# Latent attention scores: three products over 96 or 97 rows of the array become two over 128 rows and one over 33, and the small ones of two key blocks stand on the two halves of the array's rows

## Chip, core and metric

The kernel runs on one core of a Trainium2 chip. What counts is the device time of one execution, in microseconds (us); lower is better. PE is TensorE (matrix products), PEld its weight loads, ACT ScalarE, DVE VectorE, POOL GpSimd, SP the engine whose queue issues most of the DMAs (SPq).

## The reference

A trunk of two encoder layers over 2048 tokens of width 1024. The part that this case is about is the attention of the second layer (8 heads, one rotary key shared by all heads):

```
def mla_attention(q_nope, q_rope, k_nope, k_rope, v):      # per head: 64 + 32 columns, v 64
    scale = (C_NOPE + C_ROPE) ** -0.5                      # 96 ** -0.5
    ...
        s = (jnp.einsum('bqhd,bshd->bhqs', qn, k_nope)
             + jnp.einsum('bqhr,bsr->bhqs', qr, k_rope)).astype(jnp.float32) * scale
        pr = jax.nn.softmax(s, axis=-1).astype(v.dtype)
        return jnp.einsum('bhqs,bshd->bqhd', pr, v)
```

Everything around it (input projections, the windowed attention of the first layer, the gates, the output projections with layer norm) is the same in both kernels.

## The kernel before

Numbers are kept in two parts, a rounded high part (fp32r) and the rest as a low part; a product of two such numbers is high x high + high x low + low x high. `kn`, `kr`, `qn`, `qr` are the plain and the rotary columns of keys and queries in DRAM, index 0 the high part and 1 the low part.

`phase_d` is the attention. Its outer loop runs over 32 **query blocks** `blk` = head x chunk of 512 queries (four chunks to a head), its inner loop over 16 **key blocks** `kb` of 128 keys. In each key block:

- PE makes the scores of 128 keys x 512 queries in a PSUM tile `pst` (4 buffers) by three products: `kh` x `qh` with 97 rows (64 plain, 32 rotary, and a 97th row that adds minus the row maximum of the queries), `kh` x `ql` and `kl` x `qh` with 96 rows each (L1320 to L1322).
- ACT takes the exponential in place (L1323) and the rounded copy `ph` (L1326); DVE takes the rest `pl` (L1328); POOL adds `ph` to `acc`, the sum of the weights (L1334).
- PE makes one product `pm` (L1195) for the row maximum of the query block two further on, and DVE reduces it (L1196).
- PE makes the two value products `px` and `py` (L1245, L1246) of the key block `LAG` = 4 earlier.

So PE has six products of 512 columns per key block. Once in a query block come further: at `kb` = 5 the maxima of the next query block are transposed (`pmt`, L1205), turned round by ACT into `mt`, written to DRAM (`mrow`) and read back as row 96 of `qh` for the next query block (the DMA `mqh<-mrow`, last line of `mla_max_end`). The finished `px` and `py` of the query block before are copied by ACT (`oa`, `ob`) and written out (`yc`, and the last row to `sums`); `acc` of the block before is split by ACT and POOL into `acs`, summed on PE by two products `psum`, and its row `srow` goes out on SP as well.

Once in a head come the loads of the next head (`mla_load_qk`, `mla_load_v`): all go through SP's queue, in the order in which a scheduler put them there. The tiles `qh`, `ql`, `kh`, `kl` and `mv` stand twice, for even and odd heads, so these loads start when the last query block of the head before lets go of its tiles, that is at the first query block of a head, and they are for the head after it. The order of PE in `phase_d` is that of the code (`manual_schedule`); the other engines and SP's queue are put in order by the scheduler.

Of the kernel before, what the change touches and what calls it, by code (L numbers as in the profile page):

```python
# [11 lines left out]
F32 = mybir.dt.float32  # L12
F32R = mybir.dt.float32r
I32 = mybir.dt.int32
AF = mybir.ActivationFunctionType
# [5 lines left out]
P = 128  # L21
S = 2048
D = 1024
KT = D // P
CH = 512
# [4 lines left out]
LAG = 4  # L30
# [24 lines left out]
class Builder:  # L55
# [1109 lines left out]
    def _mla_qk(self, es, b, side):  # L1165
        tc, nc = self.tc, self.nc
        out = []
        for nm in ("qh", "ql", "kh", "kl"):
            p = es.enter_context(tc.tile_pool(name=f"m{nm}{b}", bufs=1, side=side))
            out.append(p.tile([97, S], F32R, name=f"m{nm}{b}"))  # L1170
        nc.scalar.activation(out[2][96:97], self.c["ones"][0:1, 0:1].broadcast_to([1, S]), AF.Copy)
        return out

    def mla_load_qk(self, h):
        d = self.d
        qh, ql, kh, kl = self.mla_qk[h % 2]
        for part, (q, k) in enumerate(((qh, kh), (ql, kl))):
            self.dma(k[0:64], d["kn"][64 * h:64 * h + 64, part])
            self.dma(k[64:96], d["kr"][:, part])
            self.dma(q[0:64], d["qn"][64 * h:64 * h + 64, part])  # L1180
            for a in range(2):
                r = 128 * (h // 4) + 64 * a + 16 * (h % 4)
                self.dma(q[64 + 16 * a:80 + 16 * a], d["qr"][r:r + 16, part])

    def mla_max(self, blk, s):

        nc, c = self.nc, self.c
        h, qc = divmod(blk, 4)
        qh, ql, kh, kl = self.mla_qk[h % 2]
# [5 lines left out]
        nc.tensor.matmul(ps, qh[0:96, q0:q0 + P], kh[0:96, kc * CH:(kc + 1) * CH], start=True, stop=True)  # L1195
        nc.vector.tensor_reduce(self.mx[blk][:, b, kc:kc + 1], ps, AX.X, ALU.max)  # L1196

    def mla_max_end(self, blk):
        nc, c = self.nc, self.c
        h, qc = divmod(blk, 4)  # L1200
# [3 lines left out]
        ps = self.psC("pmt")  # L1204
# [15 lines left out]
    def phase_d(self):  # L1220
# [9 lines left out]
        phr = Ring(es, tc, "mph", LAG + 3)  # L1230
        plr = Ring(es, tc, "mpl", LAG + 2)
        sp = es.enter_context(tc.tile_pool(name="mla", bufs=1))
        vs = self.mla_v
# [14 lines left out]
        def finish(h, qc, x, y):  # L1248
# [4 lines left out]
            ox = sp.tile([P, CH], F32, name="oa", tag="oa", bufs=2)  # L1253
            nc.scalar.activation(ox, x, AF.Copy)
            oy = sp.tile([P, CH], F32, name="ob", tag="ob", bufs=2)
# [11 lines left out]
        def total(h, qc, hl):  # L1267
# [3 lines left out]
            row = sp.tile([P, CH], F32, name="srow", tag="ob", bufs=2)[0:1]  # L1271
# [25 lines left out]
        with tc.manual_schedule(engines={mybir.EngineType.PE}):  # L1297
            for blk in range(NBLK):
                h, qc = divmod(blk, 4)
                qh, ql, kh, kl = self.mla_qk[h % 2]  # L1300
# [15 lines left out]
                for kb in range(16):  # L1316
                    with tc.high_priority(100) if blk == 0 and kb < LAG else ExitStack():
                        ps = self.ps.tile([P, CH], F32, name="pst", tag="W", bufs=4)
                        ks = slice(kb * P, (kb + 1) * P)
                        mm(ps, kh[0:97, ks], qh[0:97, qs], start=True, stop=False)  # L1320
                        mm(ps, kh[0:96, ks], ql[0:96, qs], start=False, stop=False)  # L1321
                        mm(ps, kl[0:96, ks], qh[0:96, qs], start=False, stop=True)  # L1322
# [14 lines left out]
                        if kb == MAX_AT and old is not None and blk + 1 < NBLK:  # L1337
                            self.mla_max_end(blk + 1)
                        queue.append((x, y, vs[h % 2], kb, ph, pl))
# [129 lines left out]
```

## Time and profile before

| | |
|---|---|
| median of 3 runs | 2878.97 us (2873.27 to 2884.52) |
| the profiled execution | 2881.51 us, span of its instructions 2879.7 us |
| PE busy, share of the span | 2819.8 us, 98% |
| PEld, DVE, ACT, POOL busy | 2292.0, 1987.6, 1322.2, 1096.7 us |
| mean granted TensorE clock | 0.991 |
| attention (first `pst` product to the last) | 1682.7 to 2430.9 us of the span |

"Busy" is the time in which an engine has an instruction under way. A PE product of 512 columns shows as 0.40 us, but the next one starts long before it ends, so the distance from start to start is its cost in a row of products. The clock is a share of 2.4 GHz: 1.00 is 2.4 GHz, 0.50 is 1.2 GHz.

### The profile page before, as it was taken

To read this page: it belongs to the slowest core of one execution; us is meant where nothing else is said; L and a number is where in the kernel's file an instruction comes from. 1 tells how busy PE (TensorE), PEld (TensorE's weight loads), DVE (VectorE), ACT (ScalarE), POOL (GpSimd) and SP (SyncE) were. 2 spreads that over 40 slices of the span, in tenths; PEclk is the share of its full clock that TensorE was granted. 3 is DMA by queue.
4 is the path that set the end of the run, shared out by engine and by line. 5 is a ranking of instruction groups with operands and counts; after the bars stand their busy time and mean duration, and the time that the engine had idled before them with its cause. 6 is when DMAs were issued, how large, how long until landed. Compare 5 with 4: busy or idle time off the path is not lost. (4 is left out here: it accounts for less than half of the span.)

```text
span 2879.7 us, 38354 instructions
## 1 busy us (share of the span) xinstructions
PE 2819.8 (98%) x12808; PEld 2292.0 (80%) x12808; DVE 1987.6 (69%) x3957; ACT 1322.2 (46%) x2475; POOL 1096.7 (38%) x833
## 2 busy tenths in 40 slices
PE   9999999999999999999999999999999999899999
PEld 7888888888788887888887877777777776678887
DVE  4688557786655554454764789989898995666665
ACT  3545335445211111324442368888888887211111
POOL 0011000022311111120102258898899888523432
PEclk9999999999999999999999999999999999899999
DMA  7644365453733445423873333133322323433441
GB/s 233 186 139 140 124 194 166 133 142 118 219 119 119 130 136 212 148 66 128 292 268 108 106 101 76 37 72 84 84 54 61 83 69 78 139 106 114 126 123 43
DMA packets 316598, 365.26 MB, mean 127 GB/s; under 512 B 33248, under 2 KB 244368, under 8 KB 311280
## 3 DMA queue, kind: packets, MB, share of 16 engines
q1 hardware_dynamic: 249056, 295.62, 36.6%
q10 hardware_dynamic: 67344, 67.18, 7.0%
q8 instruction: 101, 1.65, 0.2%
q14 instruction: 97, 0.79, 0.1%
HBM read 238.19 MB, written 124.53 MB: 126 GB/s over the span
## 5 line engine op out<-in xcount | busy, mean ns | idle before, releaser
L1334 POOL TENSOR_TENSOR acc<-acc,ph 128x512 f32<-128x512 f32 x448 | 582.9, 1302 | 41.8 <-ACT ph L1326 10.9
L1328 DVE TENSOR_TENSOR pl<-pst,ph 128x512 fp32r<-128x512 f32 x512 | 347.0, 684 | 62.7 <-ACT ph L1326 50.0
L1196 DVE TENSOR_REDUCE mx<-pm 128x1 f32<-128x512 f32 x512 | 347.8, 682 | 27.4 <-PE pm L1195 21.1
L78 PE MATMUL pa<-xh,w 128*128 128x512 f32 x832 | 328.4, 395 | 6.0 <-ACT xh L68 6.0
L79 PE MATMUL pa<-xl,w 128*128 128x512 f32 x832 | 329.9, 397 | 0.0
L80 PE MATMUL pa<-xh,w 128*128 128x512 f32 x832 | 328.0, 394 | 0.0
L1323 ACT ACTIVATE pst<-pst 128x512 f32<-128x512 f32 x512 | 296.6, 585 | 61.2 <-PE pst L1322 29.9
L1326 ACT ACTIVATE ph<-pst 128x512 fp32r<-128x512 f32 x512 | 301.5, 595 | 31.8 <-POOL acc L1334 1.6
L78 PE MATMUL py<-wh,ou 128*128 128x512 f32 x512 | 208.3, 407 | 13.0 <-DVE ox L639 8.2
L1320 PE MATMUL pst<-mqh,mkh 97*128 97x512 f32 x512 | 205.6, 402 | 3.6 <-DVE pl L1328 1.9
L1195 PE MATMUL pm<-mkh,mqh 96*128 96x512 f32 x512 | 203.3, 398 | 4.8 <-DVE mx L1196 4.8
L647 POOL TENSOR_TENSOR ox<-ox,ln_g 128x1024 f32<-128x1024 f32 x32 | 80.4, 2514 | 334.3 <-DMA praw<-in_pT 171.6
L90 PE MATMUL pg<-wh,oht 128*128 128x512 f32 x512 | 201.1, 393 | 4.5 <-ACT oht L68 4.5
L1245 PE MATMUL px<-ph,mv 128*128 128x512 f32 x512 | 205.3, 401 | 0.0
L79 PE MATMUL py<-wl,ou 128*128 128x512 f32 x512 | 205.3, 401 | 0.0
L1321 PE MATMUL pst<-mql,mkh 96*128 96x512 f32 x512 | 204.4, 399 | 0.0
L1322 PE MATMUL pst<-mqh,mkl 96*128 96x512 f32 x512 | 203.8, 398 | 0.0
L80 PE MATMUL py<-wh,ou 128*128 128x512 f32 x512 | 203.6, 398 | 0.0
L1246 PE MATMUL py<-pl,mv 128*66 128x512 f32 x512 | 201.9, 394 | 0.8 <-DVE pl L1328 0.7
L90 PE MATMUL pg<-wl,oht 128*128 128x512 f32 x512 | 200.4, 391 | 0.0
L671 ACT ACTIVATE osg<-pg 128x512 f32<-128x512 f32 x64 | 38.3, 599 | 344.8 <-PE pg L92 333.2
L78 PEld LDWEIGHTS pa<-xh,w 128*128 128x128 f32 x832 | 157.4, 189 | 37.8 <-ACT xh L68 7.0
(370 smaller groups left out, 6255.3 us busy)
## 6 DMA issues: line engine op xcount, KB each, us to landing
ou<-u SPq DMA_DIRECT2D x96, 256.0 KB
qw<-q SPq DMA_DIRECT2D x64, 256.0 KB
x1T<-oxt ACTq DMA_DIRECT2D x64, 256.0 KB
cx<-x1T SPq DMA_DIRECT2D x16, 1024.0 KB
q<-st SPq DMA_DIRECT2D x32, 256.0 KB
u<-ua SPq DMA_DIRECT2D x32, 256.0 KB
wraw<-in_w_out SPq DMA_DIRECT2D x16, 512.0 KB
ox<-in_x SPq DMA_DIRECT2D x16, 512.0 KB
```

The source lines that it names most:

```text
L78: mm(ps, ah, bh, start=start, stop=False)
L79: mm(ps, ah, bl, start=False, stop=False)
L80: return mm(ps, al, bh, start=False, stop=stop)
L90: mm(ps, a[:, 0, k], b[k][part][:, cols], start=k == 0 and part == 0, stop=False)
L1196: nc.vector.tensor_reduce(self.mx[blk][:, b, kc:kc + 1], ps, AX.X, ALU.max)
L1245: mm(x, v[:, kb, 0:P], ph, start=kb == 0, stop=kb == 15)
L1320: mm(ps, kh[0:97, ks], qh[0:97, qs], start=True, stop=False)
L1321: mm(ps, kh[0:96, ks], ql[0:96, qs], start=False, stop=False)
L1323: ex = nc.scalar.activation(ps, ps, AF.Exp, scale=scale)
L1326: nc.scalar.activation(ph, ps, AF.Copy)
L1328: behind = nc.vector.tensor_tensor(pl, ps, pf, ALU.subtract)
L1334: nc.gpsimd.tensor_tensor(acc, acc, pf, ALU.add)
```

## The change

The scores need 64 x 3 + 32 x 3 + 1 = 289 rows of products. The change lays them out as 128 + 128 + 33:

- `k1` x `q1`, 128 rows: plain high x high (64), rotary high x high (32), rotary low x high (32; the high rotary queries stand twice in `q1`).
- `k2` x `q2`, 128 rows: plain high x low (64), plain low x high (64).
- `k3` x `q3`, 33 rows: rotary high x low (32) and the row of minus the maximum (1). `k3` is loaded once and for all heads, even key blocks on partitions 0 to 32 and odd ones on 64 to 96. `q3` holds the 512 queries of one query block on both partition ranges, two buffers, filled by six DMAs per query block (`mla_load_q3`), two of them from `mrow`.

The key blocks are taken in pairs: both products of 128 rows of the even block, the two of 33 rows one after the other (the even block's on rows 0 to 63 of the array, the odd block's on rows 64 to 127, each in the PSUM tile of its own block), then both of the odd block. In the built program the two small ones are marked as tiles of 64 rows at row 0 and row 64, all other products of the loop as 128 rows at row 0.

To make room, the ring of `ph` goes from 7 to 6 buffers, and `oa` and `ob` (with `srow`, which shares the buffer) from two buffers to one.

```diff
     def mla_load_qk(self, h):
...
+        self.dma(k1[0:64], d["kn"][hs, 0])
+        for part in range(2):
+            self.dma(k1[64 + 32 * part:96 + 32 * part], d["kr"][:, part])
+        self.dma(q1[0:64], d["qn"][hs, 0])
+        for copy in range(2):
             for a in range(2):
                 r = 128 * (h // 4) + 64 * a + 16 * (h % 4)
-                self.dma(q[64 + 16 * a:80 + 16 * a], d["qr"][r:r + 16, part])
+                o = 64 + 32 * copy + 16 * a
+                self.dma(q1[o:o + 16], d["qr"][r:r + 16, 0])
+        for part in range(2):
+            self.dma(k2[64 * part:64 * part + 64], d["kn"][hs, part])
+            self.dma(q2[64 * part:64 * part + 64], d["qn"][hs, 1 - part])
...
+    def mla_load_q3(self, blk):
+
+        h, qc = divmod(blk, 4)
+        q3 = self.mla_q3[blk] = self.mla_q3_pool.tile([97, CH], F32R, name="mq3", tag="mq3", bufs=2)
+        for u in range(2):
+            for a in range(2):
+                r = 128 * (h // 4) + 64 * a + 16 * (h % 4)
+                o = 64 * u + 16 * a
+                self.dma(q3[o:o + 16], self.d["qr"][r:r + 16, 1, qc * CH:(qc + 1) * CH])
+            self.dma(q3[64 * u + 32:64 * u + 33], self.d["mrow"][blk])
...
-        mrow = self.d["mrow"][blk]
-        self.dma(mrow.rearrange("o (b t) -> (o b) t", b=4), mt)
-        self.dma(self.mla_qk[h % 2][0][96:97, qc * CH:(qc + 1) * CH], mrow)
+        self.dma(self.d["mrow"][blk].rearrange("o (b t) -> (o b) t", b=4), mt)
...
-        phr = Ring(es, tc, "mph", LAG + 3)
+        phr = Ring(es, tc, "mph", LAG + 2)
...
-            row = sp.tile([P, CH], F32, name="srow", tag="ob", bufs=2)[0:1]
+            row = sp.tile([P, CH], F32, name="srow", tag="ob", bufs=1)[0:1]
...
-                        ps = self.ps.tile([P, CH], F32, name="pst", tag="W", bufs=4)
-                        ks = slice(kb * P, (kb + 1) * P)
-                        mm(ps, kh[0:97, ks], qh[0:97, qs], start=True, stop=False)
-                        mm(ps, kh[0:96, ks], ql[0:96, qs], start=False, stop=False)
-                        mm(ps, kl[0:96, ks], qh[0:96, qs], start=False, stop=True)
+                        def whole(ps, kb, start):
+                            ks = slice(kb * P, (kb + 1) * P)
+                            mm(ps, k1[:, ks], q1[:, qs], start=start, stop=False)
+                            mm(ps, k2[:, ks], q2[:, qs], start=False, stop=not start)
+
+                        if kb % 2 == 0:
+                            pair = [self.ps.tile([P, CH], F32, name="pst", tag="W", bufs=4) for _ in range(2)]
+                            whole(pair[0], kb, True)
+                            for u in range(2):
+                                r = slice(64 * u, 64 * u + 33)
+                                mm(pair[u], k3[r, kb // 2], q3[r], start=u == 1, stop=u == 0)
+                            whole(pair[1], kb + 1, False)
+                        ps = pair[kb % 2]
```

PE's order in the middle of a query block. Before, one key block (`mqh`, `mql`, `mkh`, `mkl` are the tiles `qh`, `ql`, `kh`, `kl`, the number behind a name is its buffer):

```order
L1320 MATMUL pst<-mqh_13506,mkh_13514 128x512
L1321 MATMUL pst<-mql_13510,mkh_13514 128x512
L1322 MATMUL pst<-mqh_13506,mkl_13518 128x512
L1195 MATMUL pm<-mkh_14407,mqh_14399 128x512
L1245 MATMUL px<-ph_15387,mv_13637 128x512
L1246 MATMUL py<-pl_15388,mv_13637 66x512
```

And now on PE, a pair of key blocks (`mq_13506`, `mq_13510` are `q1`, `q2`; `mk_13514`, `mk_13518` are `k1`, `k2`; the row with x2 is the two small products, from `q3` and `k3`):

```order
L1354 MATMUL pst<-mq_13506,mk_13514 128x512
L1355 MATMUL pst<-mq_13510,mk_13518 128x512
L1362 MATMUL pst<-mq_14470,mk_14458 128x512 x2
L1354 MATMUL pst<-mq_13506,mk_13514 128x512
L1355 MATMUL pst<-mq_13510,mk_13518 128x512
L1226 MATMUL pm<-mk_13514,mq_13506 128x512
L1276 MATMUL px<-ph_14697,mv_13636 128x512
L1277 MATMUL py<-pl_14698,mv_13636 66x512
L1226 MATMUL pm<-mk_13514,mq_13506 128x512
L1276 MATMUL px<-ph_14708,mv_13636 128x512
L1277 MATMUL py<-pl_14709,mv_13636 66x512
```

It is twelve products for two key blocks in both, but two of the twelve are the small ones, next to each other; all scores of a pair now come before its `pm`, `px` and `py`.

SP's queue at the first query block of a head. Before (a part of the loads of the next head, the outputs of the query block just finished, and the row of maxima for the next query block):

```order
L74 DMA mql_13510<-qr 16x2048 x2
L74 DMA mv_13637<-v_94 128x16x128
L74 DMA yc<-oa 64x512 x2
L74 DMA yc<-ob 64x512
L74 DMA sums<-ob 1x512
L74 DMA mrow<-mt 4x128
L74 DMA mqh_14399<-mrow 1x512
L74 DMA sums<-srow 1x512
```

Now at the same place of SP's queue (`mq_15672` is `q3` of the next query block; `mk_13518`, `mq_13510` are `k2`, `q2` of the next head, of which the first halves stand ahead of these rows):

```order
L74 DMA yc<-oa 64x512 x2
L74 DMA yc<-ob 64x512
L74 DMA sums<-ob 1x512
L74 DMA mrow<-mt 4x128
L74 DMA mk_13518<-kn 64x2048
L74 DMA mq_13510<-qn 64x2048
L74 DMA mv_13636<-v_94 128x16x128
L74 DMA mq_15672<-mrow 1x512 x2
L74 DMA sums<-srow 1x512
```

The row is still read back behind all loads of the next head; these are now four tiles of 128 rows instead of four of 96, and the largest of them, `mv`, has moved to just ahead of the row.

POOL's order at the end of a query block. Before:

```order
L1334 TENSOR_TENSOR acc<-acc,ph_15248 128x512
L1332 TENSOR_TENSOR acc<-ph_15266,ph_15281 128x512
L69 TENSOR_TENSOR acs<-acc,acs 128x512
L1334 TENSOR_TENSOR acc<-acc,ph_15296 128x512
```

And now at POOL:

```order
L1376 TENSOR_TENSOR acc<-acc,ph_15279 128x512
L69 TENSOR_TENSOR acs<-acc,acs 128x512
L1374 TENSOR_TENSOR acc<-ph_15301,ph_15312 128x512
L1376 TENSOR_TENSOR acc<-acc,ph_15331 128x512
```

The split `acs` of the finished sum now stands ahead of the first addition of the new query block. It is so at 17 of 31 ends, against 5 of 31 before the change.

## Rows read from the trace of the kernel before

**Rows 1.** Timeline of PE, one key block: start us, us, instruction.

```profile
2100.83 0.40 PE L1320 MATMUL pst<-mqh,mkh 97*128 97x512 f32 x1
...
2102.23 0.40 PE L1320 MATMUL pst<-mqh,mkh 97*128 97x512 f32 x1
```

**Rows 2.** Two issues on SP's timeline, the same DMA of two neighbouring query blocks.

```profile
1720.84 0.21 SPq L74 DMA_DIRECT2D sums<-srow  x1
...
1743.82 0.21 SPq L74 DMA_DIRECT2D sums<-srow  x1
```

**Rows 3.** Busy time by stretch: us, then PE, PEld, DVE, ACT, POOL, clock, DMA, GB/s.

```profile
1682.00:2384.00 702.00, 695.25 (x2966) 528.65 (x2967) 636.86 (x1063) 612.92 (x1115) 626.49 (x489) 1.00 0.31 70
2009.50:2032.50 23.00, 23.00 (x101) 17.62 (x100) 21.24 (x36) 20.26 (x38) 20.69 (x17) 1.00 0.09 19
...
2383.00:2435.00 52.00, 45.39 (x177) 32.57 (x177) 27.63 (x46) 40.79 (x77) 49.43 (x40) 0.93 0.20 53
```

**Rows 4.** Timeline of PE and PEld around a transpose with four weight columns.

```profile
2389.37 0.40 PE L1322 MATMUL pst<-mqh,mkl 96*128 96x512 f32 x1
...
2389.60 0.28 PE L1205 MATMUL pmt<-ident,mxr 128*4 128x128 f32 x1
2389.60 0.19 PEld L1245 LDWEIGHTS px<-ph,mv 128*128 128x128 f32 x1
2389.63 0.48 PE L1245 MATMUL px<-ph,mv 128*128 128x512 f32 x1
2389.72 0.14 PEld L1246 LDWEIGHTS py<-pl,mv 128*66 128x66 f32 x1
2389.95 0.39 PE L1246 MATMUL py<-pl,mv 128*66 128x512 f32 x1
```

**Rows 5.** Timeline of POOL over one query block; in brackets the idle time before.

```profile
2012.96 1.29 POOL L69 TENSOR_TENSOR acs<-acc,acs 128x512 fp32r<-128x512 f32 x1 [1.18 <-ACT acs L68]
2014.22 1.29 POOL L1332 TENSOR_TENSOR acc<-ph,ph 128x512 f32<-128x512 f32 x1
2015.59 17.75 POOL L1334 TENSOR_TENSOR acc<-acc,ph 128x512 f32<-128x512 f32 x13
```

**Rows 6.** SP's timeline at the loads of a head.

```profile
1773.56 0.47 SPq L74 DMA_DIRECT2D mkh<-kn  x1
...
1784.38 7.10 SPq L74 DMA_DIRECT2D yc<-oa  x2
...
1792.70 0.25 SPq L74 DMA_DIRECT2D mrow<-mt  x1
1795.82 0.21 SPq L74 DMA_DIRECT2D mqh<-mrow  x1
```

**Rows 7.** Busy time in the query block of these loads, columns as above.

```profile
1774.30:1797.30 23.00, 23.00 (x100) 17.69 (x99) 21.34 (x36) 20.24 (x38) 20.66 (x17) 1.00 0.91 200
```

**Rows 8.** DMA issues in the attention: count, KB of each.

```profile
mkh<-kn SPq DMA_DIRECT2D x7, 512.0 KB
...
mqh<-qr SPq DMA_DIRECT2D x14, 128.0 KB
```

**Rows 9.** PE behind a head's loads, and PE's idle time ahead of products on `qh` (us, times).

```profile
1985.41 0.40 PE L1246 MATMUL py<-pl,mv 128*66 128x512 f32 x1
1986.45 0.47 PE L1320 MATMUL pst<-mqh,mkh 97*128 97x512 f32 x1 [0.64 <-DMA mqh<-mrow]
...
  DMA mqh<-mrow: 3.4, 6
```

**Rows 10.** PE and clock at the start of the attention: timeline, then busy time by stretch.

```profile
1679.85 0.27 PE L1205 MATMUL pmt<-ident,mxr 128*4 128x128 f32 x1 [1.82 <-DVE mxr L1203]
...
1681.00:1683.00 2.00, 2.00 (x10) 2.00 (x11) 1.02 (x4) 1.79 (x2) 0.00 (x0) 0.50 0.94 221
...
1685.00:1687.00 2.00, 2.00 (x6) 1.59 (x5) 1.90 (x6) 1.47 (x3) 0.00 (x0) 0.50 0.88 261
1687.00:1689.00 2.00, 2.00 (x9) 1.58 (x8) 1.63 (x4) 1.54 (x4) 1.29 (x1) 0.90 1.12 326
```

More of the change, by code (lines that the diff above doesn't have):

```diff
@@ L1165, in _mla_qk @@
     def _mla_qk(self, es, b, side):
-        tc, nc = self.tc, self.nc
         out = []
[L1168 to L1171, printed above, removed]
+        for nm in ("q1", "q2", "k1", "k2"):
+            p = es.enter_context(self.tc.tile_pool(name=f"m{nm}{b}", bufs=1, side=side))
+            out.append(p.tile([P, S], F32R, name=f"m{nm}{b}"))
         return out
@@ L1175, in mla_load_qk, with mla_rope @@
         d = self.d
[L1176 to L1180, printed above, removed]
+        q1, q2, k1, k2 = self.mla_qk[h % 2]
+        hs = slice(64 * h, 64 * h + 64)
+        self.dma(k1[0:64], d["kn"][hs, 0])
[3 more added lines that the diff above has]
+        for copy in range(2):
             for a in range(2):
                 r = 128 * (h // 4) + 64 * a + 16 * (h % 4)
-                self.dma(q[64 + 16 * a:80 + 16 * a], d["qr"][r:r + 16, part])
+                o = 64 + 32 * copy + 16 * a
[3 more added lines that the diff above has]
+            self.dma(q2[64 * part:64 * part + 64], d["qn"][hs, 1 - part])
+    def mla_rope(self, es):
+        p = es.enter_context(self.tc.tile_pool(name="mk3", bufs=1))
+        k3 = self.mla_k3 = p.tile([97, 8, P], F32R, name="mk3")
+        self.mla_q3 = {}
+        self.mla_q3_pool = p
+        kr = self.d["kr"][:, 0].rearrange("e (b u t) -> e u b t", u=2, t=P)
+        for u in range(2):
+            self.dma(k3[64 * u:64 * u + 32], kr[:, u])
+            self.nc.scalar.activation(k3[64 * u + 32:64 * u + 33],
+                                      self.c["ones"][0:1, 0:1].broadcast_to([1, 8 * P]).rearrange(
+                                          "o (b t) -> o b t", t=P), AF.Copy)
+    def mla_load_q3(self, blk):
[7 more added lines that the diff above has]
+            self.dma(q3[64 * u + 32:64 * u + 33], self.d["mrow"][blk])
     def mla_max(self, blk, s):
@@ L1194, in mla_max @@
         ps = self.psC("pm")
-        nc.tensor.matmul(ps, qh[0:96, q0:q0 + P], kh[0:96, kc * CH:(kc + 1) * CH], start=True, stop=True)
+        nc.tensor.matmul(ps, q1[0:96, q0:q0 + P], k1[0:96, kc * CH:(kc + 1) * CH], start=True, stop=True)
         nc.vector.tensor_reduce(self.mx[blk][:, b, kc:kc + 1], ps, AX.X, ALU.max)
@@ L1229, in phase_d @@
         self.mla_v[1] = self._mla_values(es, 1, "left")
-        phr = Ring(es, tc, "mph", LAG + 3)
+        phr = Ring(es, tc, "mph", LAG + 2)
         plr = Ring(es, tc, "mpl", LAG + 2)
         sp = es.enter_context(tc.tile_pool(name="mla", bufs=1))
+        self.mla_rope(es)
+        for blk in range(2):
+            self.mla_load_q3(blk)
         vs = self.mla_v
@@ L1252, in finish @@
             rows = slice(64 * (h % 2), 64 * (h % 2) + 64)
-            ox = sp.tile([P, CH], F32, name="oa", tag="oa", bufs=2)
+            ox = sp.tile([P, CH], F32, name="oa", tag="oa", bufs=1)
             nc.scalar.activation(ox, x, AF.Copy)
-            oy = sp.tile([P, CH], F32, name="ob", tag="ob", bufs=2)
+            oy = sp.tile([P, CH], F32, name="ob", tag="ob", bufs=1)
             nc.scalar.activation(oy[0:65], y[0:65], AF.Copy)
@@ L1299, in phase_d @@
                 h, qc = divmod(blk, 4)
-                qh, ql, kh, kl = self.mla_qk[h % 2]
+                q1, q2, k1, k2 = self.mla_qk[h % 2]
+                q3, k3 = self.mla_q3.pop(blk), self.mla_k3
                 qs = slice(qc * CH, (qc + 1) * CH)
@@ L1338, in phase_d @@
                             self.mla_max_end(blk + 1)
+                            if blk:
+                                self.mla_load_q3(blk + 1)
                         queue.append((x, y, vs[h % 2], kb, ph, pl))
```

4 lines of the change are left out of this document (2 added, 2 removed).

## Prediction

> **What bounds the kernel now.** I read the page first: PE is busy for 98% of the span, so only what shortens PE's row of products, or makes it wait, can show. Then PE's timeline in the attention. Six products fill one key block, from 2100.83 to 2102.23 [rows 1], that is 0.233 us from start to start; a product lasts 0.40 us there, so 0.16 us of each lies over the next. Sixteen key blocks are 22.4 us; two `psum` products (0.47) and the transpose (0.1) make 22.9 us for a query block, and the same DMA of two neighbouring query blocks is 22.98 us apart [rows 2]. An undisturbed query block is paced by PE alone.
>
> Next, the busy times by stretch. In such a query block PE has 23.00 of 23.00 us, but DVE has 21.24, POOL 20.69 and ACT 20.26 [rows 3]: all three come right behind PE. Over the first 30 query blocks the mean is 702/30 = 23.4 us and PE lacks 702 - 695.25 = 6.75 us; the last two take 52 us, with POOL at 49.43 of them and PE at 45.39 [rows 3], so POOL paces those.
>
> Last, the queries at the head loads. Six query blocks (the first of heads 1 to 6) carry the loads of a head: DMA engines at 0.91 of their time, 200 GB/s [rows 7]. SP starts the loads at 1773.56, stands 7.10 us on the `yc` issue behind them, and can issue the read-back of the row of maxima only at 1795.82 [rows 6], 22.3 us after it began. The next query block's first product needs that row; PE was held by it six times, 3.4 us in all, and in the shown case 0.64 us of a gap of 1.04 us between starts [rows 9]. So the row now lands just about when PE wants it, with nothing to spare.
>
> **What the change takes from PE.** In a pair of key blocks two of twelve products become the small ones. No row here shows two products on two halves of the array's rows, so I bound the pair of them from both sides.
>
> - Best: they run wholly at once, one 0.233 us slot is saved in each of 256 pairs: 59.7 us.
> - Worst: they don't overlap, and each change between 64-row and 128-row tiles lets the array run empty, at the 0.16 us by which a product outlasts its slot [rows 1], twice per pair: 256 x 0.33 = +84 us.
>
> Between them I go by the row that is nearest, the transpose with four weight columns, which the built program marks as a narrow tile too (32 columns). From its start to the start of `py` are 2389.95 - 2389.60 = 0.35 us, in which it and one `px` of 0.233 us run: 0.117 us for a narrow product and for both changes of tile [rows 4]. That is just the distance of the two weight loads, 2389.60 to 2389.72 = 0.12 us: a load that has nothing to hide behind costs 0.12 us, and the change of tile costs nothing that shows. The Trainium skill says otherwise, in "TensorEngine Tiling (Array Packing)", Tiling Modes: changing the mode, not just the tile, drains the engine. By the rows above a change of column tile shows no drain; no row shows a change of row tile, so the rule is a rival below.
>
> For the overlap: in the rows every weight load starts when the product before it starts [rows 4]. Taken so, the second small product starts 0.12 us after the first, when its weights are in, and the pair of them takes 0.233 + 0.12 = 0.35 us instead of 0.47. That is 0.113 us per pair, 8 x 0.113 = 0.9 us per query block: PE's part falls from 22.9 to 22.0 us. The skill, in "TensorE: Matmul & The Clock Gate", Part 3, has products on different row groups start about 4 ns apart; that would be the best case above, 59.7 us, if PE alone set the pace.
>
> **What the other engines let through.** They don't get shorter. POOL's cycle with `acs` first was 2012.96 to 2014.22, then 1.37 us to the next, then 13 additions in 17.75 us and a fourteenth at the same 1.365 us: 21.7 us, and 1.18 us of waiting for ACT's half of the split, together 22.9 [rows 5]. With the first addition ahead of `acs` that wait is covered. The change puts `acs` first at 17 of 31 ends instead of 5, so POOL can do between 21.7 and 22.9 us, in the mean about 22.3, and I let 0.2 us of PE's 0.9 be lost there, the lag being bounded now by six `ph` buffers instead of seven. ACT's 20.26 and DVE's 21.24 [rows 3] just fit. So an undisturbed query block gains 0.7 us. There are 24 of them (30 less the six with head loads): -17 us. The last two are POOL's: 0. If PE's own gain were the full 1.9 us (8 x 0.233), POOL would still hold it near 22.3, so the two cases differ by a few us only.
>
> **What the change adds.** The loads of a head grow by four times 32 rows of 8 KB (512 KB are 64 rows [rows 8]), 1.05 MB, and `q3` brings 128 KB more per query block. At 200 GB/s [rows 7] the 1.05 MB are 5.2 us in a stretch in which the DMA engines are busy already. The read-back of the row stands behind all of it, as before, and now right behind `mv`, so it lands some 5 us later; the second issue for the other half costs 0.2 us. Its `mrow` write comes earlier, so some 0.4 us of the wait for that goes away, and PE needs the row two products (0.47 us) later than before: 5.2 - 0.4 - 0.5 = 4.3. So such a query block lasts about 23.9 (22.9 and the 1 us gap) + 4.3 = 28.2 us. Six times 4.3 are +26 us. In these blocks PE's shorter row is worth nothing. On the same queue the `yc` and `sums` DMAs land late, and `srow` has only the buffer that they empty: ACT, in order, then stands for some us with all exponentials behind it; but that lies within the same wait for the row. In the 24 other query blocks the DMAs are at 0.09 of their time [rows 3], so the five more issues and the single buffers cost nothing there; without that cover each late `ob` would stop ACT.
>
> A gap of 4 to 5 us may also cost clock. At the start of the attention PE sat idle for 1.82 us and then had only small products; the granted clock then stood at 0.50 from 1681 to 1687, which is 1.2 GHz, until it came back to 2.4 GHz [rows 10]. Six us at half clock lose 3 us at most; with PE then ahead of the others I take 2, in two of the six blocks: +4 us. At most it is 6 x 3 = +18.
>
> The ones row of `kh`, 1.9 us of ACT at the start of the attention, goes away with the tile; PE's first scores wait for the transpose and `q3` there instead, so I count 0.
>
> **Sum.** -17 + 26 + 4 = +13 us on the profiled 2881.5 us, 2894.5; the median of the runs lies 2.5 us lower, so 2892 us. 0.5%, about what a measurement of this kernel can tell from no change, is 14 us. The forecast stands just inside it.
>
> **Rivals.**
>
> - *The row arrives in time.* If DMAs finish not in the order of issue, so that the small read-back passes the head's loads, or the loads start earlier, the 26 and the 4 us fall away and -17 to -25 us stay: 2857. For it: PE got the row after only 3.4 us of waiting in six cases. Against: the small `mrow` DMA needed 3.1 us to the next issue behind it [rows 6] while the loads drained. It decides as soon as the row lands within 23 us of the start of the loads.
> - *Full overlap, late rows.* PE's own gain is 1.9 us a block; POOL caps it at about 1.0: 24 x 1.0 = -24, +30: 2885.
> - *Tiles don't overlap, or the array drains.* Without overlap the 17 us are gone: 2879 + 30 = 2909. With a drain of 0.16 us at each change the pairs lose 0.21 us net (0.33 - 0.12), 8 x 0.21 x 24 = +40, and the late row lies partly under the longer blocks (1.7 us in each of six, 10 us less): 2879 + 40 + 20 = 2939. The skill's rule on mode changes would give this; the column tile speaks against it.
> - *The pair's burst.* All scores of a pair now need two of four `pst` buffers at once, and ACT gets them in bursts. If ACT falls behind, PE waits for `pl`; ACT's slack of 22.0 - 20.3 = 1.7 us per block speaks against more than some tenths.
>
> **How the numbers follow.** Forecast case (half overlap, late rows) 0.45, from 2878 to 2908; of it 0.25 within 0.5% and 0.20 slower. Row in time 0.20: 0.16 faster, 0.04 the same. Full overlap with late rows 0.10: 0.03 faster, 0.07 the same. No overlap or drains 0.25, slower but for 0.02. Sum: faster 0.19, same 0.38, slower 0.43. The range 2853 to 2925 leaves out the drains' upper end (0.12) and the lower end of rows in time (0.06).
>
> **What would show it.** The two small products' starts (0.12 us apart or a few ns) and the distance from a pair's first product to the next pair's (10 x 0.233 + 0.35 = 2.68 us if I am right, 2.57 with full overlap, 2.80 without, 3.0 with drains); PE waiting for `mq<-mrow` about 4 us at the second query block of heads 1 to 6; `srow` late there; POOL's share in the other blocks near 97%. The forecast is wrong if undisturbed blocks don't get shorter, or if PE doesn't wait for that row.

## The result and the profile after

The change made the kernel slower: median 2969.89 us (2965.09 to 2972.71) against 2876.12 us in the same session, ratio 1.0323 with an interval of 1.0307 to 1.0338. The prediction had 2892 us with a range up to 2925, so it missed the time and the range. The profiled execution took 2965.09 us, its span 2963.3 us: 83.6 us more than the span of before. The medians differ by 93.8 us: the profiled execution of before, 2881.51 us, lies above its median, the one after the change below.

First PE's timeline, one pair of key blocks after the change (start us, us, instruction; x2 are the two small products, shown as one row):

```profile
2102.12 0.39 PE L1354 MATMUL pst<-mq,mk 128*128 128x512 f32 x1
2102.35 0.40 PE L1355 MATMUL pst<-mq,mk 128*128 128x512 f32 x1
2102.67 0.50 PE L1362 MATMUL pst<-mq,mk 33*128 33x512 f32 x2
2103.11 0.50 PE L1354 MATMUL pst<-mq,mk 128*128 128x512 f32 x1
2103.45 0.40 PE L1355 MATMUL pst<-mq,mk 128*128 128x512 f32 x1
2103.69 0.39 PE L1226 MATMUL pm<-mk,mq 96*128 96x512 f32 x1
...
2105.09 0.39 PE L1354 MATMUL pst<-mq,mk 128*128 128x512 f32 x1
```

Read the distances from start to start. Away from the small products they are the 0.233 us of [rows 1]. Around them they are 0.32, 0.44 and 0.34 us. The two small products do lie over each other (0.50 us for both), but the step to them and the two steps out of them take 1.10 us where three slots would take 0.70. So a trip to the small tile costs 0.40 us and saves one slot of 0.233. From pair to pair it is 2105.09 - 2102.12 = 2.97 us; twelve slots of before are 2.80.

PEld's timeline of the same stretch says what is late (in brackets: idle before, and why):

```profile
2102.12 0.19 PEld L1355 LDWEIGHTS pst<-mq,mk 128*128 128x128 f32 x1
2102.67 0.19 PEld L1362 LDWEIGHTS pst<-mq,mk 33*128 33x128 f32 x2 [0.36 <-issue]
2103.11 0.19 PEld L1354 LDWEIGHTS pst<-mq,mk 128*128 128x128 f32 x1 [0.25 <-issue]
```

The load for `k2` starts at 2102.12, with the product before its own. The load for the small products could have started at 2102.35 in the same way, and starts at 2102.67, with its own product; so does the next one, for `k1`, at 2103.11. Loads across the change of row tile are not laid over the product before. The wait view of PEld for the attention shows it as a habit (waited for: us in total, times, longest):

```profile
PEld pst L1362 <- issue: 90.5, 242, 0.8
PEld pst L1354 <- issue: 65.0, 262, 0.4
```

Next, the waits of PE and, below them, of DVE and ACT, from 1680 to 2520 us:

```profile
PE pmt L1235 <- DVE mx L1227: 15.8, 29, 0.6
PE pm L1226 <- ACT srow L1304: 8.0, 6, 2.1
PE pm L1226 <- DVE mx L1227: 8.0, 7, 2.7
PE pst L1362 <- DMA mq<-mrow: 1.9, 2, 1.1
...
DVE rec L1312 <- DMA rec<-sums: 13.3, 5, 4.5
...
ACT srow L1304 <- DMA yc<-ob: 18.0, 6, 3.8
```

and the same waits in the kernel before:

```profile
PE pm L1195 <- DVE mx L1196: 4.8, 6, 1.5
PE pmt L1205 <- DVE mxr L1203: 1.8, 1, 1.8
PE pst L1320 <- DMA mqh<-mrow: 1.7, 3, 0.6
...
DVE rec L1281 <- DMA rec<-sums: 8.2, 4, 2.6
```

Two things are new. The transpose `pmt` waits once in nearly every query block, where before it waited once in all, at the start. And in the six query blocks with a head's loads ACT stands at `srow` for the buffer that the DMA `yc<-ob` empties; `pm`, which needs the PSUM buffer that `srow` has still to read, waits behind it. A third thing was there before and has grown: DVE stands at the reciprocal for `rec<-sums` (8.2 us before, 13.3 now), with the `pm` reductions queued behind it, and PE at `pm` for DVE (4.8 before, 8.0 now). The row of maxima holds PE as little as before: 1.9 us in two waits, 1.7 in three before. The 3.4 us in six of [rows 9] count PE and its weight loads together; half of that is PE's.

The place of the new wait at `pmt`, on PE's timeline:

```profile
1789.27 0.40 PE L1355 MATMUL pst<-mq,mk 128*128 128x512 f32 x1
1789.51 0.63 PE L1226 MATMUL pm<-mk,mq 96*128 96x512 f32 x2
1790.69 0.27 PE L1235 MATMUL pmt<-ident,mxr 128*4 128x128 f32 x1 [0.55 <-DVE mx L1227]
```

At `kb` = 4 the code makes no value products, and in a pair's order the scores of `kb` = 5 have already gone ahead of `pm`. So the `pm` of blocks 4 and 5 stand next to each other (x2), take both `psC` buffers of PSUM (`c_bufs` = 2), and `pmt`, the third to want one, waits for DVE to reduce the first. Before, three score products stood between the two `pm`.

To size these, count query blocks by the copy `oa`, one per block on ACT. By line: count, duration in ns, first and last start. The first stretch holds query blocks without head loads, the second 27 intervals, from the first to the 28th copy:

```profile
L1285 ACT ACTIVATE oa<-px x4: 597/598/618, 1713.3 to 1787.9; 128x512 f32<-128x512 f32 x4
...
L1285 ACT ACTIVATE oa<-px x28: 597/597/619, 1713.3 to 2420.4; 128x512 f32<-128x512 f32 x28
```

and the same of the kernel before:

```profile
L1254 ACT ACTIVATE oa<-px x4: 588/590/597, 1711.2 to 1779.9; 128x512 f32<-128x512 f32 x4
...
L1254 ACT ACTIVATE oa<-px x28: 587/592/599, 1711.2 to 2343.0; 128x512 f32<-128x512 f32 x28
```

An undisturbed query block went from 68.7/3 = 22.90 to 74.6/3 = 24.87 us, +1.97. Over 27 intervals it is 631.8 to 707.1 us, +75.3: 27 x 1.97 = 53.2 of it are the undisturbed length, and what the head loads add on top grew from 631.8 - 27 x 22.90 = 13.5 to 707.1 - 27 x 24.87 = 35.6, +22. The other 8 us of the span are the start of the attention (from the first `pst` to the first `oa` 34.1 us, 5.6 more than before; 29.3 in the run without a change of tile below) and small amounts elsewhere. The same two rows are taken of each experiment below; "undisturbed" and "head loads" are worked out in the same way.

### The profile page after: what moved, and what is told of

Same layout as the page of the kernel before. It is cut to its first block, busy times and chain, and to the rows that moved or that the text cites. A ratio compares the mean times of both kernels' runs of the same rounds, so it can differ in the third digit from the quotient of the medians.

```text
span 2963.3 us, 38670 instructions
## 1 busy us (share of the span) xinstructions
PE 2875.3 (97%) x12808; PEld 2227.8 (75%) x12808; DVE 1980.2 (67%) x3957; ACT 1309.4 (44%) x2475; POOL 1092.3 (37%) x833
## 5 line engine op out<-in xcount | busy, mean ns | idle before, releaser
L1354 PE MATMUL pst<-mq,mk 128*128 128x512 f32 x512 | 232.6, 454 | 0.0
L1226 PE MATMUL pm<-mk,mq 96*128 96x512 f32 x512 | 203.6, 409 | 16.1 <-ACT srow L1304 8.0
L1355 PE MATMUL pst<-mq,mk 128*128 128x512 f32 x512 | 205.4, 401 | 0.0
L79 PEld LDWEIGHTS pa<-xl,w 128*128 128x128 f32 x832 | 156.8, 188 | 31.0 <-DVE xl L69 1.5
```

The source lines that it names most:

```text
L79: mm(ps, ah, bl, start=False, stop=False)
L1226: nc.tensor.matmul(ps, q1[0:96, q0:q0 + P], k1[0:96, kc * CH:(kc + 1) * CH], start=True, stop=True)
L1354: mm(ps, k1[:, ks], q1[:, qs], start=start, stop=False)
L1355: mm(ps, k2[:, ks], q2[:, qs], start=False, stop=not start)
```

## The experiments

**Theory.** The loss is three things: the change of row tile (1.3 us per query block), `pmt` behind two `pm` (0.7), and head loads (22 us in all). **Rivals.** For the first: gaps from the order of a pair, not from the tile; or small products that don't overlap in truth. For the third: bytes, the read-back of the row, or the place on SP's queue.

**No change of tile.** Both small products over the whole array, on one pair of zero-padded tiles (the lines that make and zero these tiles are left out here):

```
-                                r = slice(64 * u, 64 * u + 33)
-                                mm(pair[u], k3[r, kb // 2], q3[r], start=u == 1, stop=u == 0)
+                                mm(pair[u], k3[0:97, kb // 2], q3[0:97], start=u == 1, stop=u == 0)
```

Expected: 

> After with the two small products as 97-row products on the whole 128-row array, so that no tile changes; rows 32 to 63 of the stacked queries are zero, and the low rotary rows of both blocks are added into each product, so the scores are not the reference's, only their timing is of use. Theory (the change of row tile costs about 0.4 us for each trip there and back: 0.320, 0.422 and 0.335 us in place of 0.233): six products at 0.233 us again, pair distance 2.80 in place of 2.97 us, 256 pairs x 0.17 = 43 us less, time 2927 (2920 to 2935). Rival (the gaps come from the order of six score products in a row, two PSUM tiles late, and not from the tile): 2970.

Measured 2923.34 us (ratio to before 1.0158, 1.0140 to 1.0177), 46.6 us less than after. PE's timeline has plain slots of about 0.233 us again:

```profile
2102.99 0.39 PE L1357 MATMUL pst<-mq,mk 128*128 128x512 f32 x1
2103.22 0.39 PE L1358 MATMUL pst<-mq,mk 128*128 128x512 f32 x1
2103.44 0.63 PE L1364 MATMUL pst<-mq,mk 97*128 97x512 f32 x2
2103.91 0.39 PE L1357 MATMUL pst<-mq,mk 128*128 128x512 f32 x1
```

and its `oa` row of four undisturbed starts:

```profile
L1288 ACT ACTIVATE oa<-px x4: 597/598/618, 1707.3 to 1778.0; 128x512 f32<-128x512 f32 x4
```

The same DMAs, the same order, two slots for the small products instead of one, and it is faster: an undisturbed block takes 70.7/3 = 23.57 us. The change of tile costs 1.30 us per block, 0.16 per pair, net of the slot that it saves.

**One trip or two.** Each small product alone behind its own block's two big ones:

```
-                            whole(pair[0], kb, True)
                             for u in range(2):
                                 r = slice(64 * u, 64 * u + 33)
-                                mm(pair[u], k3[r, kb // 2], q3[r], start=u == 1, stop=u == 0)
-                            whole(pair[1], kb + 1, False)
+                                if u == 0:
+                                    whole(pair[0], kb, True)
+                                    mm(pair[0], k3[r, kb // 2], q3[r], start=False, stop=True)
+                                else:
+                                    whole(pair[1], kb + 1, True)
+                                    mm(pair[1], k3[r, kb // 2], q3[r], start=False, stop=True)
```

Expected: 

> After with each small product alone behind its own block's two big products: two trips to the small tile in each pair of blocks, no overlap. Theory (a trip costs about 0.64 us from the end of the last big product's slot to the next big product's, whether one or two small products lie in it): pair 2.33 + 2 x 0.64 = 3.61 us in place of 2.97, 256 x 0.64 = +163 us, time about 3130 (3090 to 3150). Rival (the change of tile is free, and the pair's burst is what costs): each block has its own cadence again and the time is at most 2970, towards 2880.

Measured 3087.52 us (1.0727, 1.0707 to 1.0748), 118 more than after, below the expected 3090 to 3150 by a little. PE's timeline:

```profile
2102.42 0.40 PE L1355 MATMUL pst<-mq,mk 128*128 128x512 f32 x1
2102.74 0.50 PE L1363 MATMUL pst<-mq,mk 33*128 33x512 f32 x1
2103.17 0.50 PE L1354 MATMUL pst<-mq,mk 128*128 128x512 f32 x1
2103.51 0.40 PE L1355 MATMUL pst<-mq,mk 128*128 128x512 f32 x1
```

The `oa` row, 27 intervals:

```profile
L1285 ACT ACTIVATE oa<-px x28: 597/598/620, 1728.3 to 2534.2; 128x512 f32<-128x512 f32 x28
```

A trip with one small product has the same three steps (0.32, 0.43, 0.34) as one with two. Every block is now 805.9/27 = 29.85 us, +4.98 on the undisturbed block of after, 0.62 per pair: one more trip, 0.39, and the slot that the overlap no longer saves, 0.233. Over 32 blocks that would be 159 us; but at this length the head loads cost nothing more (the mean of all 27 intervals is that of the first four, 29.88 us), which gives 35.6 back: 124, where 118 were measured.

**Is the overlap real?** Both small products on rows 0 to 32:

```
-                                r = slice(64 * u, 64 * u + 33)
-                                mm(pair[u], k3[r, kb // 2], q3[r], start=u == 1, stop=u == 0)
+                                mm(pair[u], k3[0:33, kb // 2], q3[0:33], start=u == 1, stop=u == 0)
```

Expected: 

> After with both small products on rows 0 to 32 of the array; the odd block's small product takes the even block's rotary keys, so its scores are not the reference's. Theory (the two overlap fully, starting 3 ns apart, and the trip costs the rest): the second waits for the first, 0.233 us more per pair, 256 x 0.233 = +60 us, time about 3030 (3015 to 3040). Rival (they do not overlap in truth, their records only start together): 2970, within 5 us.

Measured 3002.34 us (1.0438, 1.0412 to 1.0464): 32 more than after, between the two numbers. The rows decide, first PE's timeline:

```profile
2104.08 0.73 PE L1361 MATMUL pst<-mq,mk 33*128 33x512 f32 x2
2104.74 0.49 PE L1354 MATMUL pst<-mq,mk 128*128 128x512 f32 x1
```

then the `oa` rows, undisturbed and over 27 intervals:

```profile
L1285 ACT ACTIVATE oa<-px x4: 597/598/618, 1713.5 to 1793.5; 128x512 f32<-128x512 f32 x4
L1285 ACT ACTIVATE oa<-px x28: 597/598/619, 1713.5 to 2450.1; 128x512 f32<-128x512 f32 x28
```

The two take 0.73 instead of 0.50 us, and an undisturbed block 80.0/3 = 26.67 us: +1.80, or 0.225 per pair, the expected slot. The overlap on two halves is real and complete. The trip is paid once, whatever lies in it: 0.39 us more than plain slots with one small product, 0.40 with two at once, and with two in a row again 0.39 (1.32 us from the last big product before them to the second one behind, where four slots take 0.93). So it isn't the few rows of a product that cost; and 96 rows next to 128 on the whole array cost nothing (`pm`: 0.24 us from the product before it, 0.23 to the next). The time grew by less than 32 x 1.80 = 58 us because the longer blocks hide part of the head loads (736.6 - 27 x 26.67 = 16.5 us instead of 35.6).

**The order of a pair alone.** The kernel before, its 97- and 96-row products as they were (the expectation speaks of 33 rows, but this kernel has no such products), both blocks' scores ahead of `pm`, `px`, `py`:

```
+                        if kb % 2 == 0:
+                            pair = [self.ps.tile([P, CH], F32, name="pst", tag="W", bufs=4) for _ in range(2)]
+                            for u in range(2):
+                                ks = slice((kb + u) * P, (kb + u + 1) * P)
+                                mm(pair[u], kh[0:97, ks], qh[0:97, qs], start=True, stop=False)
...
+                        ps = pair[kb % 2]
```

Expected: 

> Before with the order of a pair of blocks as in the change (the three products of the even block, the three of the odd one, and only then pm, px, py of both), small products still of 33 rows on the whole array. Theory (the order alone costs pmt's wait for a reduce, 12 to 20 us by the run that moved pmt): 2890 to 2897. Rival (the order is harmless and all of the loss is the change of tile and the later head loads): 2876, within 4 us.

Measured 2889.8 us against 2879.05 (1.0039, 1.0024 to 1.0054). In PE's waits the one at `pmt` is there, the same as after the change:

```profile
PE pmt L1205 <- DVE mx L1196: 16.1, 29, 0.6
```

And the `oa` rows, undisturbed and over 27 intervals:

```profile
L1254 ACT ACTIVATE oa<-px x4: 597/598/618, 1702.8 to 1773.6; 128x512 f32<-128x512 f32 x4
L1254 ACT ACTIVATE oa<-px x28: 597/598/621, 1702.8 to 2348.7; 128x512 f32<-128x512 f32 x28
```

An undisturbed block is 70.8/3 = 23.60 us, +0.70 on before and the same as in the run without a change of tile: order (0.70) and tile (1.30) together make up the 1.97. What the head loads add falls here (645.9 - 27 x 23.60 = 8.7), so the kernel loses only 11 us.

**`pmt` one product later** (after, `MAX_AT` 5 to 6):

```
-MAX_AT = 5
+MAX_AT = 6
```

Expected: 

> After with pm, pmt and the like of a block standing one product later (MAX_AT 6 in place of 5), so that pmt no longer stands right behind two pm products that hold both narrow PSUM buffers. Theory (the wait is pmt's for the reduce of the fourth block's maximum, about 0.7 us in each of 29 query blocks): the 15.8 us of waits at pmt go, pm to pmt falls from 0.945 to about 0.25-0.35 us, time 2950 (2945 to 2956). Rival (the wait only shows itself there and moves to the next PSUM or DVE wait): 2970, within 4 us of after.

Measured 2957.7 us (1.0275, 1.0258 to 1.0292), 12 less than after: the theory's direction, not its size. (The spans of the two profiled executions differ by 4.3 us only.) The wait at `pmt` is gone, but a smaller one comes in its place, the `pm` behind it, in PE's waits:

```profile
PE pm L1226 <- DVE mx L1227: 7.0, 27, 0.7
```

The `oa` row of four undisturbed starts:

```profile
L1285 ACT ACTIVATE oa<-px x4: 615/616/616, 1711.9 to 1786.0; 128x512 f32<-128x512 f32 x4
```

An undisturbed block is 74.1/3 = 24.70 us: only 0.17 of the 0.70 us come back in this stretch. The third user of the two buffers in a pair, now that `pm`, still comes late: it starts 0.60 us after the product before it (1716.76 to 1717.36) instead of 0.23. Whether a third buffer would end this was not run.

**The sums' row in a row of its own** (after, one fixed tile `ob` whose row 96 takes `srow`):

```
+        ob = sp.tile([P, CH], F32, name="ob")
-            oy = sp.tile([P, CH], F32, name="ob", tag="ob", bufs=1)
+            oy = ob
-            row = sp.tile([P, CH], F32, name="srow", tag="ob", bufs=1)[0:1]
+            row = ob[96:97]
```

Expected: 

> After with one persistent tile for the outgoing rows, whose row 96 takes the sums' row, so that the write of that row no longer waits for the DMA yc<-ob of the query block before. Theory (in the blocks with head loads the chain yc<-ob late, srow late, sums late, rec late, DVE held, pm late costs about 23 us): 10 to 25 us less, 2945 to 2960. Rival (the read-back mq<-mrow is the limit in those blocks, as the prediction had it): at most 5 us less, 2965 to 2970.

Measured 2965.39 us (1.0302, 1.0285 to 1.0318), 4.5 less than after, within the spread of its runs: the rival's number. ACT's stand at `srow` is gone and the read-back of the row takes its place, in PE's waits:

```profile
PE pmt L1235 <- DVE mx L1227: 16.0, 29, 0.6
PE pst L1364 <- DMA mq<-mrow: 10.2, 5, 3.5
```

**Both edits together**, `MAX_AT` and the fixed `ob`. Expected: 

> After with both: pmt one product later, and the sums' row in a row of its own. Theory (the two costs add up, 12 us by the run that moved pmt and 10 to 25 us by the row): 2933 to 2948. Rival (they are one wait seen twice): no faster than the better of the two alone, 2945 to 2958.

Measured 2964.89 us (1.0302, 1.0285 to 1.0320): no faster than the `pmt` edit alone, so my theory of two costs that add up fell. PE's wait for `mq<-mrow` is 21.5 us here, in six query blocks.

**All three**, these two and the whole-array small products. Expected: 

> After with all three: small products of 97 rows on the whole array (no tile changes; low rotary rows of both blocks are added, so the scores are not the reference's), pmt one product later, the sums' row of its own. Theory (the change's loss of 93 us is made of tile change, 47 us by the run on the whole array, pmt's wait and the row): 2876 to 2900. Rival (something else in the change costs, for instance the larger head loads themselves): over 2905.

Measured 2923.88 us (1.0169, 1.0145 to 1.0194), the same as with the whole-array products alone, and over the rival's 2905. PE's longest wait of the attention:

```profile
PE pst L1366 <- DMA mq<-mrow: 29.5, 6, 5.1
```

So the three runs say that several DMAs are late behind the same burst of loads: the output rows, the sums, the row of maxima. Free one and PE waits for the next. The question that was left is whether bytes or places on the queue make them late.

**Fewer bytes** (after, the rotary keys in `k1`, equal for all heads, loaded once for each buffer; 0.52 MB less per head; the loads are now a list of pieces, issued in the same order):

```
-        for part in range(2):
-            self.dma(k1[64 + 32 * part:96 + 32 * part], d["kr"][:, part])
...
+        if h < 2:
+            for part in range(2):
+                yield lambda part=part: self.dma(k1[64 + 32 * part:96 + 32 * part], d["kr"][:, part])
```

Expected: 

> After with one edit: the rotary keys in k1, the same for all heads, are loaded once for each buffer, so a head's loads shrink by 0.52 MB. Theory (the burst's bytes set how late everything behind it is): 0.52 MB at 200 GB/s are 2.6 us in each of six query blocks, 12 to 16 us less, 2954 to 2958. Rival (it is the number of DMAs and the order on SP, not the bytes): at most 4 us less, 2966 or more.

Measured 2961.8 us (1.0297, 1.0275 to 1.0319; 2952.67 to 2966.28): 8 less, between both, and its runs spread over both expectations. It settles nothing by itself.

**Another place on the queue.** The loads of a head in three parts over three query blocks, each behind the read-back of its block, and `kr` once per buffer. On the kernel before:

```
-                if qc == 1 and h + 1 < self.HEADS:
-                    self.mla_load_qk(h + 1)
-                    self.mla_load_v(h + 1)
...
+                            row = self.mla_max_end(blk + 1)
+                        if kb == MAX_AT and qc < 3 and h + 1 < self.HEADS:
+                            with tc.issue_after(row.ins) if row else ExitStack():
+                                if qc < 2:
+                                    self.mla_load_part(h + 1, qc)
+                                else:
+                                    self.mla_load_v(h + 1)
```

Expected: 

> Before with a head's loads laid out over three query blocks, each part behind the read-back mqh<-mrow of its block (first the high parts, then the low ones, then the values), and the rotary keys kr, which are the same for all heads, loaded once for each of the two buffers instead of for every head. Theory (what the six query blocks with a head's loads last beyond 22.9 us, 13 us in all, is the wait for DMAs behind that burst): 10 to 13 us less, 2864 to 2868, ratio about 0.996. Rival (the parts now make the DMAs of the sums and reciprocals late, and DVE waits there): 2877 or more.

Measured 2873.72 us against 2875.2 (0.9988, 0.9977 to 0.9998; 11 and 15 runs). The stall went as the theory says:

```profile
L1258 ACT ACTIVATE oa<-px x28: 586/592/598, 1710.5 to 2334.1; 128x512 f32<-128x512 f32 x28
```

623.6 us for 27 intervals, 8.2 less in these two profiled executions. But the medians differ by 1.5 us only, and the interval (0.6 to 6.6 us) does not reach 8.2. A part of the 8.2 is that of the one profiled execution of before: its 2881.51 us are more than any of these 15 took (up to 2881.02). The rest was not found. It is the only kernel here below before, by 0.1%.

The same edit on after with the `pmt` and `srow` edits; the parts are `k1` and `q1`, then `k2` and `q2`, then the values. Expected: 

> After with pmt one product later, the sums' row of its own, and the loads laid out as in the run on the kernel before. Theory (in the run without the new layout the six query blocks with loads last 40 us beyond the others, and all of it is the burst): 30 to 40 us less than that run, 2925 to 2935, and what is left above the kernel before is the tile change and the pair's order. Rival (larger loads cost wherever they stand): 2955 to 2965.

Measured 2941.52 us (1.0225, 1.0211 to 1.0239), 23 less than without it, short of the theory. And without a change of tile. Expected: 

> The same on the kernel whose small products go over the whole array (97 rows, low rotary rows of both blocks added, so the scores are not the reference's). Theory: no change of tile and no burst are left, only the pair's order, 0.45 us in each of 28 query blocks: 2875 to 2887. Rival (something in the change is still unaccounted for): over 2895.

Measured 2922.03 us (1.0162, 1.0148 to 1.0177): just 2 less, the theory's number missed by 40. The trace names the next in line, in DVE's waits of this last kernel:

```profile
DVE rec L1325 <- DMA rec<-sums: 27.1, 11, 3.2
```

The part with `k2` and `q2`, 2.1 MB, now stood ahead of `rec<-sums` of its own query block, and DVE, in order, stood at the reciprocals with the `pm` reductions behind it. That is the rival written down for the kernel before, and it came true here.

**Behind the last small DMA of the query block.** Four parts over four query blocks (`k1` and `q1`, `k2`, `q2`, values), each behind `rec<-sums`, `kr` again once per buffer:

```
-                            self.dma(rec, d["sums"][h, :, qs].rearrange("a (p j) -> p a j", j=4))
+                            self.rec_dma = self.dma(rec, d["sums"][h, :, qs].rearrange("a (p j) -> p a j", j=4))
...
+                        if kb == SUM_AT and h + 1 < self.HEADS:
+                            with tc.issue_after(self.rec_dma.ins) if old is not None else ExitStack():
+                                if qc < 3:
+                                    self.mla_load_part(h + 1, qc)
+                                else:
+                                    self.mla_load_v(h + 1)
```

Without a change of tile. Expected: 

> The kernel with 97-row small products (low rotary rows of both blocks added, so the scores are not the reference's), with a head's loads in four parts over four query blocks, each behind the DMA rec<-sums of its block and not ahead of it. Theory (what was left in the run with three parts is DVE waiting for rec<-sums, 27 us in 11 waits, because the loads stood ahead of it on SP): these waits go, no query block lasts over 24.5 us, 2880 to 2892, and above the kernel before there is only the pair's order. Rival (the loads' bytes cost wherever they stand, by holding up the other transfers): 2910 or more.

Measured 2879.84 us against 2876.07 (1.0011, 1.0000 to 1.0023). With it. Expected: 

> The same layout of loads on after with pmt one product later and the sums' row of its own. Theory (its seven query blocks of 25.9 to 28 us with the second part fall to 24.7): 15 to 20 us less than with three parts, 2921 to 2927, and then 28 x 1.25 = 35 us of tile change and 28 x 0.45 = 13 us of the pair's order remain above before. Rival: 2938 or more.

Measured 2921.66 us (1.0167, 1.0151 to 1.0182). The `oa` rows of the first and of the second:

```profile
L1300 ACT ACTIVATE oa<-px x28: 597/600/621, 1708.2 to 2344.1; 128x512 f32<-128x512 f32 x28
```

```profile
L1297 ACT ACTIVATE oa<-px x28: 597/598/619, 1709.8 to 2377.8; 128x512 f32<-128x512 f32 x28
```

635.9 and 668.0 us: 23.55 and 24.74 per block, and of the waits for `mq<-mrow` and `rec<-sums` a single one of 0.5 us is left in the two together. With the waits went the slow clock: over these intervals the granted clock is 1.00 in both, where it was 0.98 right after the change. The bytes are those of the runs with three parts, which took 42 and 20 us more, so it wasn't the bytes but their place on the queue that cost (`k2` and `q2` are also two parts now instead of one; place and size of a part were not run apart).

The last two runs differ in the small products alone (and their zero padding), and the packed one is 41.8 us slower: 0.163 us for each of 256 pairs, the price seen on PE's timeline. The one without a change of tile stands within 0.3% of before, but two terms cancel there: its 27 intervals are 12.3 us longer than those of before with its own loads laid out (635.9 against 623.6), 0.46 us per block that are left of the pair's order, while before pays 13.5 us at its head loads. Of the 93.8 us that the change cost, then, 48.2 go with the place of the loads and the small edits beside it (2969.89 to 2921.66), 41.8 with the tile, and 3.8 are left.

## Why the prediction was wrong

**Half overlap at 0.35 us for the small pair, -17 us: the step that failed.** "The change of tile costs nothing that shows" was read from the transpose [rows 4], whose tile is narrower in columns; the new products change the tile in rows. There the runs show 0.40 us per trip, against one slot of 0.233 saved: 1.30 us more per query block, 35 us over 27, where the forecast had a gain of 17. The overlap, which I took to be half, is whole. So the rival of tiles that drain was right in kind and near in size: it had 0.33 us of drains less 0.12 of half an overlap, 0.21 per pair; measured are 0.40 less a whole slot of 0.233, 0.16. The Trainium skill's rule in "TensorEngine Tiling (Array Packing)", Tiling Modes, that a change of mode drains the engine, agrees with the row tile's 0.32, 0.44 and 0.34 us; I had set it aside on the evidence of another kind of change. No run here tells whether the array itself drains or the late weight load is all of the price.

**What the other engines let through: not reached.** POOL never became the limit, since PE's blocks grew (it was busy for 20.53 of 24.90 us in one without loads).

**The pair's order: a cost that I did not see.** I looked for ACT falling behind in the pair's burst and found slack enough, which was so. The narrow PSUM buffers did not come up: two `pm` next to each other and `pmt` behind them, 0.70 us in each query block, 19 us over 27. In the profile of before it could be worked out: DVE's reductions and two `psC` buffers stood in the code, and the new order of PE shows three users in a row.

**Head loads, +26 us and 4 of clock: near in size by luck, wrong in place.** The blocks with loads cost 22 us more than before, clock included. PE waited for the row only 1.9 us; `srow`, which I had put "within the same wait", and `rec`, which I had not named, came first. The path was misread in the profile of before already: of the 3.4 us that I took for PE held by the row, PE's are 1.7, while it waited 4.8 us at `pm` for DVE, once in each of the six blocks. The row is next behind `srow` and `rec`, as the runs without the `srow` wait show (10 to 30 us at `mq<-mrow`). That it also depends on the length of the blocks can be seen from 35.6, 16.5 and about 0 us at 24.9, 26.7 and 29.9 us per block.

The size came from two errors against each other. PE's waits in these blocks are 17.9 us (8.0, 8.0 and 1.9) against 6.5 before (4.8 and 1.7): 11 more, where I had 26. And the granted clock fell in three of the six blocks, to 0.50, which is 1.2 GHz:

```profile
1813.00:1826.00 13.00, 11.52 (x26) 6.79 (x27) 8.48 (x16) 5.68 (x11) 5.17 (x5) 0.50 0.17 38
2120.00:2126.50 6.50, 6.50 (x15) 4.07 (x16) 3.76 (x6) 4.17 (x8) 4.51 (x4) 0.50 0.79 191
2338.50:2345.00 6.50, 6.41 (x15) 4.05 (x16) 4.73 (x11) 2.29 (x5) 3.78 (x3) 0.50 0.03 7
```

It fell at waits of 2.72 and of 2.12 us at a `pm`, and behind three of 0.7 to 1.1 us close together; before the change it stood at 1.00 through all these blocks. Of the 26 us at half clock at most 13 are lost, where I had 4.

**The sum.** Forecast +13 on the span, measured +83.6: 17 + 35 = 52 from the tile, 19 from the order, 22 - 30 = -8 from the head loads (the waits far less than forecast, the clock more), and 8 from the start of the attention and outside the query blocks, which I had at nothing. The 42 us that the packed products cost in the last two runs are the same tile term, over all 32 blocks.

**The signs named.** A pair of 2.97 us was the sign given for drains (3.0), and small products a few ns apart the one for full overlap: both came. "The forecast is wrong if undisturbed blocks don't get shorter" is what happened, and the other condition nearly did: PE waited for the row 1.9 us in two waits, not about 4 in each of six blocks.

## What to carry to other kernels

Products on a smaller tile of the array's rows must save more than the trip there and back: here a trip cost 0.40 us, 1.7 slots of 512 columns, and saved one; two small products per trip can't pay for it, however well they overlap. A price read from one kind of tile change says nothing of another. When the order of the products on PE changes, count the users of each set of PSUM buffers in the new order, and when a burst of loads holds up one small DMA, look which small DMA is next before taking the first wait away: moving the burst behind the last of them is what helped.

## What the runs showed of the hardware that was not expected

Two 33-row products on rows 0 to 32 and 64 to 96 run wholly at once, 3 ns apart in their starts (0.50 us for both, 0.50 for one alone, 0.73 for two on the same rows). Across a change of row tile the weight load starts with its own product instead of the one before, and the first big product after the small ones also stands longer (0.50 us instead of 0.40). A change of column tile, at the transpose [rows 4], showed nothing of its own: the weight load behind it starts with the transpose, and the 0.48 us of the next product, with 0.32 to the one after it, come behind transposes on the whole array too (in the kernel before, 0.48 at 107.36 us and 0.32 to the next).
